# Up projection of a decoder block on one core: where the second 1/rms lives, and the order of some products and evictions

## The chip, the cores and the metric

One core of a Trainium2 chip runs the whole kernel in one launch. The metric is the device time of that launch in microseconds; where several runs are shown, their median counts. A profile is one execution of its own, with its own time, and its trace begins at the first instruction. TensorE (PE) multiplies, VectorE (DVE), ScalarE (ACT) and GpSimd (POOL) do the element-wise work, and SyncE (SP) issues most of the transfers. All matrix data are 32-bit floats, held for the products as a rounded high part and a low part.

## The reference, cut to what matters

```
x  = x + g1 * mix                                  # (1024 tokens, 1024 features)
h2 = rmsnorm(x, norm2_g) * (1 + sc2) + sh2         # 1/rms over the features of each token
u  = h2 @ w_up                                     # 1024 -> 2 * 2816
u  = causal_dwconv(u, conv_ffn_w)                  # 3 taps along the tokens
ff = silu(gate) * val                              # u split in two halves of 2816
x  = x + g2 * (ff @ w_down)
```

Everything ahead of the first line (a short convolution and an attention, merged by gates, and the product `mix` itself) has been done by other stages; the change lies between the end of `mix` and the first blocks of `u`.

## The kernel before

Activations are kept transposed: features on the 128 partitions (8 feature tiles, ND = 8, in two groups of NK = 4), tokens along the row, in two halves of 512 (`lo` and `hi`). A product of two 32-bit operands is three products of their parts: high by high, high by low, low by high. So one output block of 128 by 512 over 4 feature tiles is 12 products of TensorE.

**The output projection.** `mix_mm(e, w, halves)` (L1400) sums the product of feature tile e in an accumulator, and `mix_end(m)` (L1406) evicts it: one DVE instruction adds it, times the gate, to `x1[e]`, ACT squares the result, POOL adds the square to a running sum `sqs` (for the last feature tile, e = 7, the square stays in a tile of its own, `sq7`), and SP stores `x1[e]` to DRAM. For e = 4 to 7 the first token half is done first and the second half after it, so that the norm of the first half runs beside the products of the second.

**The norm of one half.** `norm2_sum` (L1422) sums the squares over the features: 8 products with one column of ones (16 entries on TensorE), then four small DVE and ACT instructions for 1/rms, and four that write diagonal matrices `diag`. `norm2_spread` (L1434) multiplies ones by them (4 products, 8 entries), which leaves 1/rms of each token on all partitions in a PSUM bank `pb`. `norm(e, g, pb)` (L1439) scales `x1[e]` in place by it, and `split_h` on ACT (L1444) and `split_l` on DVE (L1450) make the high and low part of the operand. The operands of the first half are B11 and B21, of the second B12 (its tile is named T4, since T4 takes its place later) and B22. `h2_chain` (L1494) does norm and split of the first half step by step, between the evictions of `mix`.

**The up projection.** Output tiles of 128 features come in pairs, a gate and a value block per `Up` object: `u.g` and `u.v`, each an accumulator of two PSUM banks (1024 columns). The first three, u0, u1 and u2, use plain products: `u.plain(n, half)` (L1577) is one block of 12 products; bit 0 of n says gate or value, bit 1 which group of feature tiles. From the fourth on a scheme with seven products in place of eight is used; its operands T1 to T3 are made by `t_sums` and `t_op` (L1716, L1726) on DVE and ACT while TensorE works on the plain products, and T4 (in the place of B12) when u2 has read B12. Weight tiles are fetched by `up_fetch` and split in high and low by `plain_split` (L1516): ACT writes `wh`, DVE `wl`. Splits 0 and 1 (`wsp[0:2]`) are u0's gate and value, 2 and 3 u1's, 4 and 5 u2's.

**What sets the order.** For PE, DVE, ACT and POOL the order of the instructions is that of the program text (a `manual_schedule` block); each engine takes its own in that order. SP's transfers are ordered by the scheduler. PSUM is eight banks, all of them held by `acc4` (L1291): four buffers of two banks, taken in rotation, and a new tile in a buffer waits until the last user of the old one is done. The 1/rms of the second half has no buffer of its own: before the change it lies in the `hi` half of u1.v,

```
    pst = pb = u1.v[:, hi]
```

and u1's products for the first token half, which write `u1.v[:, lo]`, come in the program ahead of the loop that reads `pb`.

Of the kernel before, what the change touches and what calls it, by code (L numbers as in the profile page):

```python
# [33 lines left out]
def tile_hybrid_block(  # L34
# [51 lines left out]
    def wsplit(fetched, eng=vector, pool=None):  # L86

        ws, n, m = fetched
        if pool:
            wh, wl = (pool.tile([P, 1040], F32R, tag=nm, name=nm, bufs=2) for nm in ("wh", "wl"))  # L90
        else:
            wh, wl = wtile("wh"), wtile("wl")
        scalar.activation(wh[:, : n * m], ws[:, : n * m], AF.Copy)  # L93
        eng.tensor_tensor(out=wl[:, : n * m], in0=ws[:, : n * m], in1=f32(wh[:, : n * m]), op=ALU.subtract)  # L94
        return tuple(t[:, : n * m].rearrange("p (n m) -> p n m", n=n) for t in (wh, wl))
# [5 lines left out]
    def mac(acc, wh, wl, xh, xl, halves, start, stop):  # L101

        n = 512
        terms = ((wh, xh), (wh, xl), (wl, xh))
        for t, (w, xx) in enumerate(terms):
            for hf in halves:
                sl = slice(hf * n, hf * n + n)
                mm(acc[:, sl], w, xx[:, sl], start=start and t == 0, stop=stop and t == 2)
# [36 lines left out]
    NK = ND // 2  # L145
    lo, hi = slice(0, 512), slice(512, 1024)
# [15 lines left out]
    def newton_rsqrt(pool, v, n, nm, root_of=None):  # L162


        s = pool.tile([P, n], F32, tag="nr_s", name=nm + "s", bufs=2)
        y = pool.tile([P, n], F32, tag="nr_y", name=nm + "y", bufs=2)
        t = pool.tile([P, n], F32, tag="nr_t", name=nm + "t", bufs=2)
        r = pool.tile([P, n], F32, tag="nr_r", name=nm + "r", bufs=2)
        if root_of:
            scalar.activation(s, root_of[0], AF.Sqrt, scale=root_of[1], bias=epst)  # L170
        else:
            scalar.activation(s, v, AF.Sqrt)
        vector.reciprocal(y, s)
        vector.scalar_tensor_tensor(out=t, in0=v, scalar=-0.5, in1=y, op0=ALU.mult, op1=ALU.mult)
        vector.tensor_tensor(out=t, in0=t, in1=y, op=ALU.mult)
        vector.scalar_tensor_tensor(out=r, in0=t, scalar=1.5, in1=y, op0=ALU.add, op1=ALU.mult)
        return r
# [406 lines left out]
    def small(nm):  # L584
        return bp.tile([P, NT * NH], F32, name=nm)

    z = zf.rearrange("p a b -> p (a b)")
    nz, u, w, lw, m, num, den, lf = (small(n) for n in "nz u w lw m num den lf".split())
# [702 lines left out]
    def acc4(nm):  # L1291
        return psD.tile([P, S], F32, tag="acc", name=nm, bufs=4)
# [50 lines left out]
    wmix = {}  # L1343
# [56 lines left out]
    def mix_mm(e, w, halves, ks=range(ND), acc=None):  # L1400
        acc = acc or acc4("mix")
        for k in ks:
            mac(acc, w[0][:, k, :], w[1][:, k, :], mH[:, k, :], mL[:, k, :], halves, k == 0, k == ND - 1)
        return e, acc, halves

    def mix_end(m):  # L1406

        e, acc, halves = m
        sl = slice(512 * halves[0], 512 * halves[-1] + 512)
        vector.scalar_tensor_tensor(out=x1[e][:, sl], in0=acc[:, sl], scalar=g1[:, e : e + 1], in1=x1[e][:, sl],  # L1410
                                    op0=ALU.mult, op1=ALU.add)
        for g in halves:
            src = x1[e][:, hsl[g]]
            if e in (0, ND - 1):
                scalar.activation(sq7 if e else sqs[g], src, AF.Square)
            else:
                sq = ep.tile([P, 512], F32, tag="sq", name="sq", bufs=2)
                scalar.activation(sq, src, AF.Square)
                gpsimd.tensor_tensor(out=sqs[g], in0=sqs[g], in1=sq, op=ALU.add)
        sync.dma_start(x1_d[e, :, sl], x1[e][:, sl])  # L1420

    def norm2_sum(g, pst):  # L1422

        for i in range(4):
            for t, sq in enumerate((sqs[g], sq7)):
                mm(pst[:, i : i + 1], sq[:, i * P : (i + 1) * P], ones[:, 0:1], start=t == 0, stop=t == 1)
        v = up.tile([P, 4], F32, tag="v2", name="v2", bufs=2)
        vector.tensor_scalar(out=v, in0=pst[:, 0:4], scalar1=1.0 / D, scalar2=EPS, op0=ALU.mult, op1=ALU.add)
        r = newton_rsqrt(up, v, 4, "r2")
        for i in range(4):  # L1430
            vector.tensor_scalar(out=diag[:, i * P : (i + 1) * P], in0=ident, scalar1=r[:, i : i + 1], scalar2=None,
                                 op0=ALU.mult)

    def norm2_spread(pb):  # L1434

        for i in range(4):
            mm(pb[:, i * P : (i + 1) * P], ones, diag[:, i * P : (i + 1) * P], start=True, stop=True)
# [12 lines left out]
    def split_l(dst, kk, src, bias=None, eng=vector):  # L1450
        if bias is None:
            eng.tensor_tensor(out=dst[1][:, kk], in0=src, in1=f32(dst[0][:, kk]), op=ALU.subtract)
        else:
            vector.scalar_tensor_tensor(out=dst[1][:, kk], in0=src, scalar=bias, in1=f32(dst[0][:, kk]), op0=ALU.add,
                                        op1=ALU.subtract)
# [11 lines left out]
    for e in range(4):  # L1467
        if e < 2:
            m = mix_mm(e, wmix[e], (0, 1), (ND - 2, ND - 1), ms[e][1])
        else:  # L1470
            m = mix_mm(e, wmix[e], (0, 1))
# [7 lines left out]
    def up_fetch():  # L1479

        n = len(raw)
        raw.append(wfetch(kview(w_up[0], (n // 2 + n % 2 * NF) * P, P), 8, P))

    for e in range(4, ND):
        m = mix_mm(e, wmix[e], (0,))
# [8 lines left out]
    def h2_chain():  # L1494

        for e in range(ND + 2):
            if e < ND:
                norm(e, 0, pb)
            if 1 <= e <= ND:
                d = e - 1  # L1500
                t, bias = x1[d][:, lo], b2[:, d : d + 1]
                if d < NK:
                    split_h(B11, d, t, bias)
                else:
                    scalar.activation(t, t, AF.Identity, bias=bias)
                    split_h(B21, d - NK, t)
            if e >= 2:
                d = e - 2
                t, bias = x1[d][:, lo], b2[:, d : d + 1]
                if d < NK:  # L1510
                    split_l(B11, d, t, bias)
                else:
                    split_l(B21, d - NK, t)
            yield

    def plain_split():  # L1516

        wsp.append(wsplit(raw[len(wsp)]))
        if len(raw) < 2 * N0:
            up_fetch()  # L1520

    wsp = []
    m = mix_mm(4, wmix[4], (1,), range(4))
    norm2_sum(0, acc4("st"))
    m = mix_mm(4, wmix[4], (1,), range(4, ND), m[1])
    pb = acc4("pb")[:, lo]
    norm2_spread(pb)
    mix_end(m)
    chain = h2_chain()
    m = mix_mm(5, wmix[5], (1,))  # L1530
# [4 lines left out]
        next(chain)  # L1535
    mix_end(m)
    m = mix_mm(6, wmix[6], (1,))
    for _ in chain:
        pass
    plain_split()  # L1540
    mix_end(m)
    m = mix_mm(7, wmix[7], (1,))
    plain_split()
    mix_end(m)
    eS.close()
    xbS.close()
    mS.close()
# [184 lines left out]
    def norm_low(e):  # L1732
        split_l((B12, B22)[e // NK], e % NK, x1[e][:, hi], b2[:, e : e + 1])

    u0, u1, u2 = U[:N0]
    for u in (u0, u1):
        u.v, u.g = (acc4(nm) for nm in ("upv", "upg"))
    u0.xs = wsp[0:2]
    pst = pb = u1.v[:, hi]
    u0.plain(0, 0)  # L1740
    plain_split()
    u1.xs = wsp[2:4]
    norm2_sum(1, pst)
    u0.plain(1, 0)
    u0.plain(2, 0)
    norm2_spread(pb)
    u0.plain(3, 0)
    for n in range(4):
        u1.plain(n, 0)
    for e in range(ND):  # L1750
        norm(e, 1, pb)
        split_h((B12, B22)[e // NK], e % NK, x1[e][:, hi], b2[:, e : e + 1])
        if e:
            norm_low(e - 1)
    norm_low(ND - 1)
    for n in (0, 2, 1, 3):
        u0.plain(n, 1)
    for n in (0, 1, 2, 3):
        u1.plain(n, 1)
    for kk in range(NK):  # L1760
# [20 lines left out]
            u0.ff_out()  # L1781
            U[3].fetch(up)
    u2.xs = wsp[4:6]
    u2.v, u2.g = (acc4(nm) for nm in ("upv", "upg"))
    for n in (0, 2, 1, 3):
        for half in range(2):
            u2.plain(n, half)
# [16 lines left out]
    for f in range(N0, NF):  # L1804
        u, bf = U[f], U[f - 1]
# [69 lines left out]
    class Step:  # L1875
# [40 lines left out]
        def mm(self, banks, es=range(4)):  # L1916
            for e in es:
                es_ = slice(e * P, (e + 1) * P)
                for t, (i, j) in enumerate(((0, 0), (0, 1), (1, 0))):
                    mm(banks[e], self.A[i][:, es_], self.B[j], start=self.p in FIRST and self.c == 0 and t == 0,  # L1920
                       stop=self.c == NC - 1 and t == 2, skip_group_check=True)
# [55 lines left out]
    u = U[NF - 1]  # L1977
# [8 lines left out]
    for t, st in enumerate(steps[: len(steps) - NE + 1]):  # L1986
        n = t // NC
# [81 lines left out]
```

## Time and profile before

| | us |
|---|---|
| median of 3 runs (1484.1, 1484.42, 1488.18) | 1484.42 |
| the profiled execution, whole | 1484.04 |
| its span, from the first to the last instruction | 1482.3 |
| TensorE busy | 1405.8 (95%) |
| VectorE busy | 1101.4 (74%) |
| ScalarE busy | 652.7 (44%) |
| GpSimd busy | 503.9 (34%) |

The mean granted TensorE clock is 0.989 of full speed. The stretch that the change touches runs from about 770 us (the last evictions of `mix`) to about 860 us (the first products of u2). A row of a timeline gives the start, the duration, the engine, the line, the operation, the tiles, and in brackets the idle time of the engine before it with the instruction that released it. Matmuls overlap: the pace is the distance of their starts, not their duration.

### The profile page before, as it was taken

The numbers are of one execution on the slowest core, as the hardware profiler recorded it, in microseconds if no ns is written. First come the engines' busy times: TensorE is split into PE (matmuls) and PEld (weight loads), VectorE is DVE, ScalarE is ACT, GpSimd is POOL, SyncE is SP. The second block draws the span as 40 slices with busy tenths as digits, with TensorE's granted clock in tenths as the row PEclk, the third lists the DMA queues.
The fourth block names the chain that finished last, engine by engine and source line by source line (L and its number), as shares of the span: only waits on it lengthen the run. The fifth ranks groups of instructions, "written<-read, shape, count | busy, mean of one in ns | idle before, by whom it ended". The sixth has DMA issues, their size and how long they took to land. (4 is left out here: it accounts for less than half of the span.)

```text
span 1482.3 us, 19374 instructions
## 1 busy us (share of the span) xinstructions
PE 1405.8 (95%) x6668; PEld 1155.2 (78%) x6668; DVE 1101.4 (74%) x1828; ACT 652.7 (44%) x1104; POOL 503.9 (34%) x532
## 2 busy tenths in 40 slices
PE   5889789999999999899999899999999999999997
PEld 4679668887888888678787677888888888888875
DVE  7965798987777776457745678778777786898764
ACT  6454453434555454555323343333333333444443
POOL 3646566655555553313121013333333331000000
PEclk9999999999999999999999999999999999999999
DMA  9539654537655557675952032222222213983622
GB/s 285 158 113 329 194 148 128 151 94 205 162 159 126 147 133 250 193 272 205 240 138 86 0 100 86 85 86 86 85 85 72 70 44 109 390 317 106 214 79 72
DMA packets 260760, 222.45 MB, mean 150 GB/s; under 512 B 43117, under 2 KB 213445, under 8 KB 260661
## 3 DMA queue, kind: packets, MB, share of 16 engines
q1 hardware_dynamic: 259389, 218.61, 49.2%
q0 software_dynamic: 1136, 2.56, 0.6%
q8 instruction: 53, 0.87, 0.3%
q14 instruction: 46, 0.38, 0.1%
q10 hardware_dynamic: 136, 0.04, 0.0%
HBM read 169.76 MB, written 51.41 MB: 149 GB/s over the span
## 5 line engine op out<-in xcount | busy, mean ns | idle before, releaser
L1920 PE MATMUL dn<-bL,aH 128*128 128x512 f32 x308 | 120.3, 391 | 0.6 <-DVE bL L1914 0.6
L1920 PE MATMUL dn<-bH,aH 128*128 128x512 f32 x308 | 120.9, 392 | 0.0
L1920 PE MATMUL dn<-bH,aL 128*128 128x512 f32 x308 | 120.0, 390 | 0.0
L1557 ACT ACTIVATE wh<-ws 128x512 fp32r<-128x512 f32 x95 | 55.5, 627 | 133.7 <-POOL ws L1591 130.9
L730 DVE TENSOR_TENSOR ol<-ws,oh 128x512 fp32r<-128x512 f32 x98 | 94.8, 976 | 14.6 <-ACT oh L729 11.3
L94 DVE TENSOR_TENSOR wl<-ws,wh 128x1024 fp32r<-128x1024 f32 (+1 forms) x51 | 69.5, 1363 | 41.3 <-ACT wh L93 41.3
L729 ACT ACTIVATE oh<-ws 128x512 fp32r<-128x512 f32 x98 | 61.3, 626 | 71.6 <-PE pacc L775 38.4
L1591 POOL TENSOR_TENSOR ws<-ws 128x512 f32<-128x512 f32 x19 | 24.6, 1293 | 195.0 <-DVE wl L94 195.0
L1162 ACT ACTIVATE L<-L,mn 128x256 f32<-128x256 f32 (+6 forms) x56 | 46.5, 830 | 60.4 <-DVE mn L1160 58.5
L1165 POOL TENSOR_SCALAR L<-L,rs 128x384 f32<-128x384 f32 (+7 forms) x62 | 48.7, 786 | 70.2 <-DVE rs L1164 68.5
L1920 PEld LDWEIGHTS dn<-bL,aH 128*128 128x128 f32 x308 | 57.8, 188 | 13.8 <-DVE bL L1914 2.0
L1185 ACT ACTIVATE th<-pt 128x512 fp32r<-128x512 f32 (+1 forms) x80 | 43.8, 551 | 56.2 <-PE pt L1179 54.5
L559 POOL TENSOR_TENSOR ws<-ws 128x512 f32<-128x512 f32 x42 | 55.1, 1311 | 36.4 <-DVE ol L730 16.9
L1920 PEld LDWEIGHTS dn<-bH,aH 128*128 128x128 f32 x308 | 57.8, 188 | 12.3 <-ACT bH L1913 0.4
L1920 PEld LDWEIGHTS dn<-bH,aL 128*128 128x128 f32 x308 | 57.8, 188 | 11.9
L93 ACT ACTIVATE wh<-ws 128x1024 fp32r<-128x1024 f32 (+1 forms) x58 | 60.8, 1051 | 13.3 <-DMA ws<-in_w_branch_a_dram 5.1
L1558 DVE TENSOR_TENSOR wl<-ws,wh 128x512 fp32r<-128x512 f32 x76 | 64.2, 863 | 2.3 <-ACT wh L1557 2.3
L1913 ACT ACTIVATE aH<-dws 128x512 fp32r<-128x512 f32 x52 | 32.8, 631 | 74.6 <-issue 41.0
L1186 DVE TENSOR_TENSOR tl<-pt,th 128x512 fp32r<-128x512 f32 (+1 forms) x80 | 50.5, 634 | 18.8 <-ACT th L1185 17.4
L1678 DVE SCALAR_TENSOR_TENSOR u<-upv,cwT,u 128x1023 f32<-128x1023 f32 (+1 forms) x44 | 56.4, 1281 | 10.7 <-ACT u L1674 10.0
L439 POOL TENSOR_TENSOR wacc<-wacc,wa 128x256 f32<-128x256 f32 x48 | 43.3, 903 | 56.0 <-ACT wa L438 53.0
L1914 DVE TENSOR_TENSOR aL<-dws,aH 128x512 fp32r<-128x512 f32 x52 | 35.8, 689 | 34.3 <-ACT aH L1913 34.3
(564 smaller groups left out, 4506.9 us busy)
## 6 DMA issues: line engine op xcount, KB each, us to landing
wa<-in_w_ada_dram SPq DMA_DIRECT2D x48, 512.0 KB
dws<-in_w_down_dram SPq DMA_DIRECT2D x96, 256.0 KB
ws<-in_w_up_dram SPq DMA_DIRECT2D x44, 512.0 KB
ws<-in_w_in_dram SPq DMA_DIRECT2D x36, 512.0 KB
ff<-ff_d SPq DMA_DIRECT2D x44, 256.0 KB
ff_d<-u SPq DMA_DIRECT2D x21, 512.0 KB
xt<-in_x_dram SPq DMA_DIRECT2D x8, 512.0 KB
v_d<-vt SPq DMA_DIRECT2D x8, 512.0 KB
```

Of the source, the lines that this page charges most:

```text
L93: scalar.activation(wh[:, : n * m], ws[:, : n * m], AF.Copy)
L94: eng.tensor_tensor(out=wl[:, : n * m], in0=ws[:, : n * m], in1=f32(wh[:, : n * m]), op=ALU.subtract)
L559: gpsimd.tensor_tensor(out=o, in0=a, in1=b, op=ALU.subtract)
L729: scalar.activation(h, src, AF.Copy)
L730: eng.tensor_tensor(out=l, in0=src, in1=f32(h), op=ALU.subtract)
L1162: scalar.activation(L[:, :n], L[:, :n], AF.Exp, scale=-1.0, bias=mn, accum_out=sm)
L1165: eng.tensor_scalar(out=L[:, :n], in0=L[:, :n], scalar1=rs, scalar2=0.0, op0=ALU.mult, op1=ALU.add)
L1186: vector.tensor_tensor(out=flat[2][:, c0:], in0=flat[0][:, c0:], in1=f32(flat[1][:, c0:]), op=ALU.subtract)
L1557: scalar.activation(ops[0][:, sl], src, AF.Copy)
L1558: eng.tensor_tensor(out=ops[1][:, sl], in0=src, in1=f32(ops[0][:, sl]), op=ALU.subtract)
L1678: vector.scalar_tensor_tensor(out=u[:, s:], in0=acc[:, : S - s], scalar=cwT[:, 2 - s, n : n + 1], in1=u[:, s:], op0=ALU.mult, op1=ALU.add)
L1920: mm(banks[e], self.A[i][:, es_], self.B[j], start=self.p in FIRST and self.c == 0 and t == 0, stop=self.c == NC - 1 and t == 2, skip_grou ...
```

## The change

The second half's 1/rms gets an accumulator of its own, `norm_ps`: the sum goes to its first bank, the spread to its second. It takes the next buffer of the rotation, so u1.v becomes the fifth tile and shares the buffer of `norm_ps`. The loop that normalises the second half stands directly behind the spread, with the fourth weight split inside it (after its sixth feature tile). u0's blocks for the second half come ahead of the two blocks that write u1.v's first half, and in the order 0, 1, 2, 3. Gate and value tiles are created in the other order. At the end of `mix`, the eviction of feature tile 6 comes after three steps of the chain and not at its end, and the eviction of tile 7 ahead of the third weight split.

```diff
     m = mix_mm(6, wmix[6], (1,))
+    for _ in range(3):
+        next(chain)
+    mix_end(m)
     for _ in chain:
         pass
     plain_split()
+    m = mix_mm(7, wmix[7], (1,))
     mix_end(m)
-    m = mix_mm(7, wmix[7], (1,))
     plain_split()
-    mix_end(m)
...
     u0, u1, u2 = U[:N0]
-    for u in (u0, u1):
-        u.v, u.g = (acc4(nm) for nm in ("upv", "upg"))
-    u0.xs = wsp[0:2]
-    pst = pb = u1.v[:, hi]
+    norm_ps = acc4("pb")
+    u0.g, u0.v, u1.g, u1.v = (acc4(nm) for nm in ("upg", "upv", "upg", "upv"))
+    u0.xs, u1.xs = wsp[0:2], wsp[2:3]
     u0.plain(0, 0)
-    plain_split()
-    u1.xs = wsp[2:4]
-    norm2_sum(1, pst)
+    norm2_sum(1, norm_ps[:, lo])
     u0.plain(1, 0)
-    u0.plain(2, 0)
+    pb = norm_ps[:, hi]
     norm2_spread(pb)
-    u0.plain(3, 0)
-    for n in range(4):
-        u1.plain(n, 0)
     for e in range(ND):
         norm(e, 1, pb)
         split_h((B12, B22)[e // NK], e % NK, x1[e][:, hi], b2[:, e : e + 1])
         if e:
             norm_low(e - 1)
+        if e == NK + 1:
+            plain_split()
+            u1.xs = wsp[2:4]
     norm_low(ND - 1)
-    for n in (0, 2, 1, 3):
+    u0.plain(2, 0)
+    u0.plain(3, 0)
+    u1.plain(0, 0)
+    u1.plain(2, 0)
+    for n in (0, 1, 2, 3):
         u0.plain(n, 1)
+    u1.plain(1, 0)
+    u1.plain(3, 0)
     for n in (0, 1, 2, 3):
         u1.plain(n, 1)
...
-    u2.v, u2.g = (acc4(nm) for nm in ("upv", "upg"))
+    u2.g, u2.v = (acc4(nm) for nm in ("upg", "upv"))
```

## Rows read from the trace of the kernel before

**Rows 1.** The page, busy time of TensorE: us, share of the span, instructions.

```profile
PE   1405.8 (95%) x6668; PEld 1155.2 (78%) x6668; DVE 1101.4 (74%) x1828; ACT 652.7 (44%) x1104; POOL 503.9 (34%) x532
```

**Rows 2.** Windows: length, busy us of each engine, granted clock, DMA share, GB/s.

```profile
776.50:778.30 1.80, 1.80 (x18) 1.75 (x17) 0.00 (x0) 0.19 (x1) 0.00 (x0) 1.00 0.00 0
...
801.40:804.90 3.50, 1.89 (x17) 1.80 (x16) 1.86 (x3) 1.57 (x2) 0.00 (x0) 0.99 0.66 196
804.90:808.10 3.20, 3.20 (x10) 2.52 (x10) 2.15 (x10) 0.21 (x1) 0.00 (x0) 0.50 0.84 262
812.00:827.00 15.00, 15.00 (x70) 12.05 (x68) 0.00 (x0) 0.00 (x0) 0.00 (x0) 1.00 0.00 1
827.00:838.80 11.80, 7.78 (x26) 4.10 (x26) 11.45 (x18) 5.73 (x9) 0.00 (x0) 1.00 0.00 0
```

**Rows 3.** Waits of TensorE, 798 to 860 us: us, times, longest.

```profile
PE upv L1426 <- ACT U L1415: 1.6, 1, 1.6
PE upg L1567 <- ACT T4H L1448: 1.6, 1, 1.6
...
PE upg L1567 <- DVE wl L94: 0.3, 1, 0.3
```

**Rows 4.** Timeline of TensorE, both norm sums and the plain products.

```profile
776.57 0.28 PE L1426 MATMUL st<-ones,sqs 128*128 128x1 f32 x2
...
778.28 0.48 PE L108 MATMUL mix<-mH,wh 128*128 128x512 f32 x1
...
781.16 1.05 PE L1437 MATMUL pb<-U,ones 128*128 128x128 f32 x8
781.96 0.48 PE L108 MATMUL mix<-mH,wh 128*128 128x512 f32 x1
...
798.61 0.39 PE L1567 MATMUL upg<-B11H,wh 128*128 128x512 f32 x1
...
801.40 0.28 PE L1426 MATMUL upv<-ones,U 128*128 128x1 f32 x2
...
804.92 0.77 PE L1567 MATMUL upv<-B11H,wh 128*128 128x512 f32 x1
...
809.31 0.39 PE L1567 MATMUL upg<-B21H,wh 128*128 128x512 f32 x1
...
826.62 0.40 PE L1567 MATMUL upv<-B21H,wl 128*128 128x512 f32 x1
...
838.77 0.40 PE L1567 MATMUL upv<-T4H,wh 128*128 128x512 f32 x1
...
855.37 0.39 PE L1567 MATMUL upg<-B11H,wh 128*128 128x512 f32 x1
...
858.71 0.39 PE L1567 MATMUL upg<-T4H,wh 128*128 128x512 f32 x1
```

**Rows 5.** Timeline of VectorE: a weight split, two evictions, the second norm.

```profile
785.39 1.22 DVE L94 TENSOR_TENSOR wl<-ws,wh 128x1024 fp32r<-128x1024 f32 x1 [0.42 <-ACT wh L93]
...
797.92 0.75 DVE L1410 SCALAR_TENSOR_TENSOR x<-mix,mod,x 128x512 f32<-128x512 f32 x1
...
801.84 0.74 DVE L1410 SCALAR_TENSOR_TENSOR x<-mix,mod,x 128x512 f32<-128x512 f32 x1
...
806.59 0.87 DVE L1431 TENSOR_SCALAR U<-ident,r2r 128x128 f32<-128x128 f32 x4
827.05 1.41 DVE L1442 SCALAR_TENSOR_TENSOR x<-x,a,upv 128x512 f32<-128x512 f32 x2 [19.59 <-PE upv L1567]
...
836.52 1.63 DVE L1454 SCALAR_TENSOR_TENSOR B22L<-x,mod,B22H 128x512 fp32r<-128x512 f32 x2
```

**Rows 6.** Timeline of ScalarE: a weight split, and the start of T4.

```profile
784.32 1.04 ACT L93 ACTIVATE wh<-ws 128x1024 fp32r<-128x1024 f32 x1
...
870.74 2.69 ACT L1446 ACTIVATE T4H<-x 128x512 fp32r<-128x512 f32 x4 [11.52 <-PE upv L1567]
```

**Rows 7.** Timeline of SP's queue: the store of x1[7], second half.

```profile
802.61 0.35 SPq L1420 DMA_DIRECT2D x_d<-x  x1
```

## The prediction, made before the changed kernel was run

> **What bounds the kernel now.** I read the page first: TensorE is busy 95% of the span [rows 1], so only what lets TensorE stand or run slowly can be won. Then its waits in the stretch of the change, then its timeline there, and last the timelines of the engines that release it. Between 798 and 860 us it waits for the last square, for the first T4 part, for the parts after it, and for a weight split [rows 3]. The pace of its undisturbed products comes from one row pair: from 838.77 to 855.37 there are six blocks of 12, 72 products, in 16.60 us, 0.2306 us each, so 2.77 us a block [rows 4].
>
> Three places of this stretch are slower than that.
>
> First, the second sum of squares. Its products begin at 801.40 and stand until the square of feature tile 7 is there [rows 3]; u0's next block begins at 804.92, 3.52 us later [rows 4]. The first half's sum is the same work with nothing to wait for: 776.57 to 778.28, 1.71 us [rows 4]. The square is late because its eviction is: DVE evicts tile 6 at 797.92 and tile 7 at 801.84 [rows 5], although TensorE had ended tile 7 when u0 began at 798.61 [rows 4]. In the program's order a weight split stands ahead of each.
>
> Second, the clock: right after that stretch it is granted at 0.50, the 1.2 GHz level, from 804.9 to 808.1 [rows 2], and the block from 804.92 to 809.31 takes 4.39 us [rows 4].
>
> Third, the second norm. The diagonals are ready at 806.59 + 0.87 = 807.46, but DVE stands 19.59 us until 827.05, released by a product into upv [rows 5]. The last product into u1.v's `lo` half starts at 826.62 and takes 0.40 [rows 4]: 827.02. So the read of `pb`, which was complete long before, waits for products into the other bank of the same tile. When it goes, the products of the second half follow DVE one feature tile at a time: two blocks, 24 products, hold TensorE from 826.62 + 0.23 = 826.85 to 838.77 [rows 4], with 7.78 us busy of 11.80 [rows 2].
>
> **The change part by part.** No product, split or transfer is added or removed; everything is order and place. The sum is made in the profiled execution (span 1482.3, whole time 1484.04, 0.38 under the median of the runs, 1484.42).
>
> *The evictions of mix.* Tile 6's eviction now comes after three chain steps, tile 7's ahead of the third split. Tile 6 moves ahead of the chain's last low part and the second split (ACT 1.04, DVE 1.22 [rows 5, 6]); that split moves behind tile 6's square, about 0.8 us later, and is first needed by u0's second block at 803. Tile 7 can be evicted when its products end, about 798.8; with the eviction (0.74) and the square (before, the eviction ended at 802.58 and the sum's 1.71 us, counted back from 804.92, began at 803.21: 0.63) it is there by 800.2, and the sum starts at 801.40: a margin of 1.2 us. The wait goes: 3.52 − 1.71 = **−1.81 us**. If tile 7 came as late as before, this term would be 0, and nothing makes it worse than before. Split 3 now follows the square and is ready about 802.7; u1's first block needs it at 812.
>
> *The clock.* Without the stand, sum, one block and spread are what the first half had: 1.71 us, 12 products in 2.88 (778.28 to 781.16), spread 0.80 (to 781.96) [rows 4], and the clock was 1.00 over that sum [rows 2]. I take the first half's block: 4.39 − 2.88 = **−1.51 us**. The other end is 0 (the clock falls again).
>
> *The spread with one block ahead of it and not two.* The chain from sum to diagonals took 807.46 − 804.92 = 2.54 us [rows 4, 5], the block takes 2.88: the cover is 0.34 us thinner than I would like, but it holds. The fourth split, which stood ahead of this chain on ACT and DVE, is no longer there. Without that cover the price is the missing part, between 0 and 2.54; the first half, with exactly this order, has no gap. I take 0.
>
> *The norm loop.* It now stands behind the spread alone. TensorE's new times: sum 801.40 to 803.11, block to 805.99, spread to 806.79, four more blocks for the first half (one starts 0.08 late after the spread, as 2.88 against 2.77 shows) to 817.95; then u0's second half: its T4 blocks from 817.95, its first B22 block from 823.49, its end at 829.03; u1's six remaining blocks to 845.65. DVE starts the loop at 805.99 + 1.05 = 807.04. Before, the loop ran from 827.05 to 836.52 + 1.63 = 838.15, 11.10 us or 1.39 a feature tile [rows 5]. The four T4 pairs are thus ready about 807.1 + 5 × 1.39 = 814, four us before use. The fourth split inside the loop, with ACT idle and then DVE, costs at most 1.04 + 1.22 = 2.26 [rows 5, 6], so the loop ends by 820.4, three us before the first B22 block. If those covers were gone, TensorE would pay the missing part us by us. u1.v must wait for the loop (same buffer): 820.4 against its first block at 829.03. So the paced stretch becomes two plain blocks: 838.77 − 826.85 = 11.92 against 24 × 0.2306 = 5.53, **−6.39 us**.
>
> *Behind it.* The T1 to T3 work on DVE and ACT begins 838.15 − 820.4 = 17.7 us earlier, while u2's first block begins 9.7 earlier. That block took 858.71 − 855.37 = 3.34 us, since it met a split not yet ready [rows 3, 4]; with eight us more lead that goes: 3.34 − 2.77 = **−0.57 us**. The next thing on ACT, T4, waits for TensorE's reading of B12 (11.52 us idle before 870.74 [rows 6]), so from there all engines move with TensorE, and the small waits after it stay as they are. U[3]'s fetch waits for the buffer of the fourth split, which comes free some 12 us later than before (about 817 against 805), and its first readers come after T4, which is to start near 860: a cover of over 40 us. Gate and value tiles in the other order only exchange which buffer is free first.
>
> Sum: −1.81 − 1.51 − 6.39 − 0.57 = **−10.28 us**: 1473.8 for the profiled execution, **1474.1** as a median.
>
> **Rivals.**
>
> *The clock still falls at the second sum.* For it: it fell here once [rows 2], and 1.7 us of one-column products remain. Against: the same sum in the first half left it at 1.00 [rows 2]. Price 1.51: 1475.7. The Trainium skill ("TensorE: Matmul & The Clock Gate", Part 1, "What's actually happening") says that "the default state is throttled, and activity releases the throttle"; by that a dull stretch is enough, even without a stand, and the time would be this rival's; the trace shows one case either way.
>
> *The loop still waits for products, by whatever rule the wait was made.* If norm were released only after the fourth block behind the spread, at 818.4 and not 807.1, it would end at 818.4 + 11.10 + 2.26 = 831.8, u0's first B22 block about 0.7 later, at 832.5 and not 826.26. That loses 6.2 of the 10.28: 1480.3. For it: the 19.59 us. Against: in the new program no product stands between spread and loop.
>
> *Slower: the store of x1[7].* The loop overwrites x1[7] in place, so it must wait until the store of its second half has read it. Before, the store was issued at 802.61 [rows 7] and the overwrite came about 836; now 799.6 and about 818.3. A store landing at X puts the B22 block's end at about X + 2.8; from X = 823.5 it costs time, from X = 833.7 (34 us after its issue) it eats the whole gain, and at 40 us the time would be 1490. For it: SP's order is the scheduler's and may put weight loads ahead. Against: DMA share is 0.00 from 812 to 827 [rows 2], so all had landed within 9.4 us.
>
> *The wait only changes its place,* because the DVE and ACT work behind the loop, not the loop, ends last: then u2 begins where it did, 1484.4. Against: DVE is idle those 19.59 us, and the change gives them to exactly this work.
>
> **How the numbers follow.** Forecast 0.82 (1474.1), clock 0.10 (1475.7), late loop 0.04 (1480.3), wait moved 0.01 (1484.4), store 0.03 (1490). A measurement tells about 0.3%, 4.45 us, from no change: faster means under 1479.97. The first two are faster, 0.92; the next two within, 0.05; the last slower, 0.03. The range: at the low end the forecast less 1.8 us, for runs that differ and for small waits behind 860 that I left as they are; at the high end the clock rival and as much again: 1472.3 to 1477.5.
>
> **What would show it.** Right: no wait of TensorE at the second sum; granted clock 1.00 throughout from 798 to 860; DVE's first norm of the second half right behind the spread, near 807; no wait for T4 or B22 parts; u2's first product near 845.6; and everything behind it moved by one amount, about 10.3. Wrong: a new wait of TensorE in front of the spread, in front of u1.v's first block or for the third or fourth split, or 0.50 after the sum. The forecast fails if the DVE loop starts after 811 (its margin of four us gone), or if the time won by 846 is lost again behind 860.

## The result, and the profile after

The changed kernel takes 1473.59 us (median of 4 runs, 1471.79 to 1476.64) against 1484.26 of the kernel before in the same rounds (median of 4). The ratio is 0.9925, with a 95% interval of 0.9908 to 0.9942: between 8.6 and 13.7 us less. The forecast was 1474.1 in a range of 1472.3 to 1477.5.

| profiled execution | before | after |
|---|---|---|
| whole | 1484.04 | 1473.5 |
| span | 1482.3 | 1471.5 |
| TensorE busy | 1405.8 | 1403.4 |

The busy time of TensorE hardly changed (2.4 us): most of what went is time in which it stood. Up to the change the two executions agree by luck: the second sum of squares begins at 801.40 before and at 801.38 after, so the two timelines can be laid on each other by their times. Here is TensorE's timeline of the changed kernel, from that sum to u2's second block; it answers to the second half of [rows 4]. The row of the kernel before in which the sum stood is given ahead of it.

```profile
803.29 1.77 PE L1426 MATMUL upv<-ones,U 128*128 128x1 f32 x14 [1.61 <-ACT U L1415]
```

```profile
801.38 1.84 PE L1426 MATMUL pb<-ones,U 128*128 128x1 f32 x16
803.09 0.48 PE L1569 MATMUL upv<-B11H,wh 128*128 128x512 f32 x1
...
805.94 1.05 PE L1437 MATMUL pb<-U,ones 128*128 128x128 f32 x8
806.75 0.48 PE L1569 MATMUL upg<-B21H,wh 128*128 128x512 f32 x1
...
817.90 0.40 PE L1569 MATMUL upg<-T4H,wh 128*128 128x512 f32 x1
...
829.05 0.39 PE L1569 MATMUL upv<-B11H,wh 128*128 128x512 f32 x1
...
845.74 0.39 PE L1569 MATMUL upg<-B11H,wh 128*128 128x512 f32 x1
...
848.54 0.39 PE L1569 MATMUL upg<-T4H,wh 128*128 128x512 f32 x1
```

All 16 entries of the sum now stand in one row without a gap (before there were 2, a stand, and 14). The block behind it takes 805.94 − 803.09 = 2.85 us and not 4.39. u0's second half begins at 817.90 and u2 at 845.74 (855.37 before). The windows of the same stretch, with columns as in [rows 2]:

```profile
801.40:803.20 1.80, 1.80 (x18) 1.80 (x17) 1.23 (x1) 0.02 (x1) 0.00 (x0) 1.00 0.99 314
803.20:806.00 2.80, 2.80 (x14) 2.29 (x14) 1.71 (x9) 0.20 (x1) 0.00 (x0) 1.00 0.69 210
806.00:818.00 12.00, 12.00 (x58) 9.96 (x57) 9.75 (x14) 5.63 (x8) 0.00 (x0) 1.00 0.01 2
818.00:829.00 11.00, 11.00 (x49) 8.90 (x48) 10.63 (x17) 4.57 (x7) 0.00 (x0) 1.00 0.17 48
```

The first two numbers of each row are equal: TensorE is busy all the time. The granted clock (third number from the right) is 1.00 throughout. VectorE's timeline shows why; it answers to [rows 5]: the two evictions, the diagonals, the loop's first norm and its last low parts.

```profile
795.15 0.74 DVE L1410 SCALAR_TENSOR_TENSOR x<-mix,mod,x 128x512 f32<-128x512 f32 x1
...
799.07 0.74 DVE L1410 SCALAR_TENSOR_TENSOR x<-mix,mod,x 128x512 f32<-128x512 f32 x1
...
804.50 0.88 DVE L1431 TENSOR_SCALAR U<-ident,r2r 128x128 f32<-128x128 f32 x4
807.03 1.41 DVE L1442 SCALAR_TENSOR_TENSOR x<-x,a,pb 128x512 f32<-128x512 f32 x2 [1.65 <-PE pb L1437]
...
818.81 1.62 DVE L1454 SCALAR_TENSOR_TENSOR B22L<-x,mod,B22H 128x512 fp32r<-128x512 f32 x2
```

The loop is released by the spread (line 1437 into pb) after 1.65 us of idle time, in place of 19.59 and a product into upv. Both evictions come 2.8 us earlier. From 740 to 1300 us, into the down projection, these waits of TensorE are left (total, times, longest), besides one of 0.3 us in the down projection:

```profile
PE upv L1569 <- ACT s L1633: 1.3, 1, 1.3
PE upv L1569 <- ACT wh L93: 0.9, 1, 0.9
PE upg L1569 <- DVE U L1625: 0.6, 1, 0.6
PE upv L1569 <- DVE wl L1560: 0.6, 1, 0.6
PE upv L1569 <- DVE wl L94: 0.5, 1, 0.5
```

They are those that the kernel before had behind T4; all waits of [rows 3] are gone.

### The profile page after: what moved, and what is told of

Same layout as the page of the kernel before. It is cut to its first block, busy times and chain, and to the rows that moved or that the text cites. A ratio compares the mean times of both kernels' runs of the same rounds, so it can differ in the third digit from the quotient of the medians.

```text
span 1471.5 us, 19375 instructions
## 1 busy us (share of the span) xinstructions
PE 1403.4 (95%) x6668; PEld 1155.1 (78%) x6668; DVE 1099.4 (75%) x1828; ACT 651.8 (44%) x1104; POOL 504.1 (34%) x532
## 5 line engine op out<-in xcount | busy, mean ns | idle before, releaser
L1680 DVE SCALAR_TENSOR_TENSOR u<-upv,cwT,u 128x1023 f32<-128x1023 f32 (+1 forms) x44 | 56.4, 1282 | 10.7 <-ACT u L1676 9.9
```

What stands on the lines that cost most here:

```text
L1680: vector.scalar_tensor_tensor(out=u[:, s:], in0=acc[:, : S - s], scalar=cwT[:, 2 - s, n : n + 1], in1=u[:, s:], op0=ALU.mult, op1=ALU.add)
```

## The experiments

The time of one execution differs by some us from the next, and most of it ahead of the change: in the ten profiles of the table below the second sum begins between 797.98 and 803.73 us. So beside the ratio of whole times I give the length of the affected stretch in each profile: from the first product of the second sum to the first product with bL in the down projection. For before and after it is read from the sum's row (801.40 in [rows 4], 801.38 above) and the first time in these two rows, of before and of after (durations shortest, median and longest in ns, then first and last start):

```profile
L1920 PE MATMUL dn<-bL,aH x308: 387/389/504, 1252.0 to 1474.6; 128*128 128x512 f32 x154
```

```profile
L1925 PE MATMUL dn<-bL,aH x308: 387/389/504, 1242.0 to 1464.9; 128*128 128x512 f32 x154
```

| kernel | median us | ratio to before (95%) | stretch us | against before |
|---|---|---|---|---|
| before | 1484.4 and 1483.9 | 1 | 450.6 | |
| after | 1473.59 | 0.9925 (0.9908 to 0.9942) | 440.6 | −10.0 |
| after, again | 1474.30 | 0.9928 (0.9913 to 0.9944) | 440.6 | −10.0 |
| 1: evictions only | 1481.39 | 0.9979 (0.9966 to 0.9991) | 447.3 | −3.3 |
| 2: norm only | 1477.64 | 0.9953 (0.9935 to 0.9970) | 444.0 | −6.6 |
| 3: shared tile | 1474.73 | 0.9934 (0.9915 to 0.9953) | 440.6 | −10.0 |
| 4: loop two blocks earlier | 1477.20 | 0.9954 (0.9940 to 0.9968) | 445.6 | −5.0 |
| 5: no block under the root | 1477.15 | 0.9950 (0.9935 to 0.9964) | 443.9 | −6.7 |
| 6: work ahead of T4 | 1467.25 | 0.9881 (0.9861 to 0.9900) | 434.9 | −15.7 |
| 7: split 4 ahead | 1473.39 | 0.9924 (0.9902 to 0.9946) | 440.6 | −10.0 |

Each ratio is taken to the kernel before in the same rounds: 1484.26 for the first row of the changed kernel, 1484.4 for experiments 1 to 4, 1483.9 for 5 to 7 and the changed kernel again.

My theory was that three causes add up: the late square, the low clock that the stand in front of it brings, and the loop's wait for products that have nothing to do with it.

**The changed kernel again**, as the measure of the others.

> The changed kernel once more, on the chip and in the rounds of the other three, as their measure: 10 to 10.7 us less than before, and in its profile 440.6 us from the first product of the second sum to the first product of the down projection.

The stretch is 440.6 again (799.78 to 1240.4); the whole time is 9.6 us under before in those rounds, a little less than the 10 to 10.7 expected, which lie within its interval (8.3 to 12.9). The stretch repeats to a tenth of a us where the whole time does not; that is why the experiments are read by it.

**1: the evictions alone.** The kernel before, with

```diff
     m = mix_mm(6, wmix[6], (1,))
+    for _ in range(3):
+        next(chain)
+    mix_end(m)
     for _ in chain:
         pass
     plain_split()
+    m = mix_mm(7, wmix[7], (1,))
     mix_end(m)
-    m = mix_mm(7, wmix[7], (1,))
     plain_split()
-    mix_end(m)
```

> The kernel before with the new order of the last mix evictions alone; the second 1/rms still lies in u1.v. Theory (three separate causes that add up): the square of tile 7 comes before the sum, so the stand of 1.6 us goes, and with it the stretch at clock 0.50, since it was the stand that let the clock fall: 1.81 + 1.51 = 3.3 us less than before. DVE still waits some 19.6 us for the loop, and the paced stretch of 11.92 us stays. Rival (the one-column products alone let the clock fall): 0.50 stays after the sum, 1.8 us less. Rival (the stretch is bound by the loop's wait, so that what is won ahead of it is lost in it): no change.

The stretch is 3.3 us shorter, as the theory had it. In TensorE's timeline the sum is one row, and VectorE still waits in front of the loop, 17.83 us and not the 19.6 expected, since the products that hold it now end earlier behind the sum:

```profile
803.73 1.84 PE L1426 MATMUL upv<-ones,U 128*128 128x1 f32 x16
```

```profile
826.03 1.40 DVE L1442 SCALAR_TENSOR_TENSOR x<-x,a,upv 128x512 f32<-128x512 f32 x2 [17.83 <-PE upv L1569]
```

The clock behind the sum, as a window:

```profile
805.40:808.60 3.20, 3.20 (x16) 2.64 (x16) 2.40 (x10) 0.21 (x1) 0.00 (x0) 1.00 0.79 234
```

It is 1.00, where the kernel before had 0.50 for the same products. So the first rival, that the one-column products alone let the clock fall, is out, and with it the prediction's reading that a dull stretch is enough even without a stand; and what was won ahead of the loop's wait was not lost in it.

**2: the norm alone.** The changed kernel with the old order of the evictions (the diff of experiment 1 taken back).

> The changed kernel with the old order of the last mix evictions. Theory: the stand in front of the second sum (1.6 us) and the clock of 0.50 behind it are back, so block u0(1,0) takes about 4.4 us again; the loop still starts right behind the spread, and the paced stretch is gone. Against before 10.1 - 3.3 = 6.8 us less. Rival (the evictions are needed for the loop to be in time): TensorE waits for T4 or B22 parts and less than 5 us is won.

6.6 us, against 6.8 expected; with the 3.3 of experiment 1 that makes 9.9 of the 10.0. The stand is back, and the clock with it:

```profile
802.74 1.72 PE L1426 MATMUL pb<-ones,U 128*128 128x1 f32 x14 [1.64 <-ACT U L1415]
```

```profile
804.40:807.50 3.10, 3.10 (x9) 2.44 (x9) 1.70 (x9) 0.21 (x1) 0.00 (x0) 0.52 0.36 127
```

TensorE waits for no T4 or B22 part: the loop is in time without the evictions. The two hunks are independent.

**3: the tile of its own taken away.** The changed kernel with

```diff
-    norm_ps = acc4("pb")
     u0.g, u0.v, u1.g, u1.v = (acc4(nm) for nm in ("upg", "upv", "upg", "upv"))
+    norm_ps = u1.v
```

> The changed kernel with the 1/rms of the second half in u1.v as before (sum in its first bank, spread in its second), all orders as in the change: no tile of its own. Theory (what holds the loop is the products into the same tile that stand ahead of it in the program; behind the loop they do no harm): same as the changed kernel, 10 us less than before, the loop starts near 807 us. Rival (the tile of its own is what frees the loop): DVE waits again for products into upv, about 820 or later, TensorE waits for T4 and B22 parts, and at most 4 us less than before is left.

The stretch is that of the changed kernel to a tenth, and the loop starts right behind the spread, though it reads from upv:

```profile
803.63 1.41 DVE L1442 SCALAR_TENSOR_TENSOR x<-x,a,upv 128x512 f32<-128x512 f32 x2 [1.65 <-PE upv L1437]
```

The rival falls: with the new order, the tile of its own gives no time. What frees the loop is that it stands ahead of the blocks that write u1.v. The other way round, a tile of its own with the loop left in its old place, was not run.

**4: the loop only two blocks earlier.** The kernel before, 1/rms in u1.v, with

```diff
-    for n in range(4):
+    for n in (0, 2):
         u1.plain(n, 0)
     for e in range(ND):
         norm(e, 1, pb)
...
     norm_low(ND - 1)
+    for n in (1, 3):
+        u1.plain(n, 0)
     for n in (0, 2, 1, 3):
         u0.plain(n, 1)
```

> The kernel before, 1/rms still in u1.v, with one move: the loop stands ahead of the two blocks that write u1.v, but still behind three blocks into other tiles (u0(3,0), u1(0,0), u1(2,0)). It tells by which rule the loop waited. Theory (by tile): the loop starts right behind the spread, near 813.2, runs beside those three blocks, and the first block into u1.v waits until the loop's last read, near 822.8, 1.5 us after TensorE could have begun it; u2 begins near 850.5 and 5.4 us less than before are measured. Rival (by place in the program: whatever product stands ahead holds it): the loop starts near 821.3, TensorE stands for the whole loop (some 9.8 us), and the kernel is about 3 us slower than before.

The loop is released by the spread although three blocks into other tiles stand between the two in the program, and the first block into u1.v waits for the loop's last read, by the 1.5 us expected:

```profile
811.57 1.41 DVE L1442 SCALAR_TENSOR_TENSOR x<-x,a,upv 128x512 f32<-128x512 f32 x2 [5.73 <-PE upv L1437]
```

```profile
819.37 0.39 PE L1567 MATMUL upg<-B21H,wl 128*128 128x512 f32 x1
821.28 0.47 PE L1567 MATMUL upv<-B11H,wh 128*128 128x512 f32 x1 [1.52 <-DVE x L1442]
821.58 0.39 PE L1567 MATMUL upv<-B11L,wh 128*128 128x512 f32 x1
```

5.0 us are won, 5.4 were expected. The starts around this wait lie 1.91 apart and the next two 0.30, where undisturbed products are 0.23 apart: the wait cost 1.91 − 0.23 + 0.07 = 1.75 and not 1.5, which is 0.2 of the missing 0.4; the rest was not followed. So the waits of this program go by the tile, in both directions: in the kernel before the read waited 19.59 us for products that stand ahead of it into the other bank of its PSUM tile, and here a product waited 1.52 us for reads of the other bank. Place in the program alone does not hold the loop, and the kernel did not become slower.

**5: nothing beside the chain to the diagonals.** The changed kernel with

```diff
     norm2_sum(1, norm_ps[:, lo])
-    u0.plain(1, 0)
     pb = norm_ps[:, hi]
     norm2_spread(pb)
+    u0.plain(1, 0)
```

> The changed kernel with the spread directly behind the sum of squares: block u0(1,0), which lay beside the chain from the sum to the diagonals, comes after the spread. Theory (the block covers the chain; a stand among such small products lets the clock fall): TensorE stands some 1.7 us in front of the spread, the clock is granted at 0.50 for some 3 us after it, and the kernel takes 3.2 us more than the changed one. Rival (the clock fell in the kernel before for another reason): it stays at 1.00, and 1.7 us more are measured.

The stretch is 3.3 us longer than the changed kernel's, 3.2 were expected. TensorE stands 1.62 us in front of the spread, and the next block runs at half the clock:

```profile
806.89 1.59 PE L1437 MATMUL pb<-U,ones 128*128 128x128 f32 x8 [1.62 <-DVE U L1431]
```

```profile
808.10:810.80 2.70, 2.70 (x8) 2.16 (x8) 2.15 (x4) 1.38 (x2) 0.00 (x0) 0.50 0.00 0
```

**7: the fourth split back ahead of the sum.** The changed kernel with

```diff
     u0.plain(0, 0)
+    plain_split()
+    u1.xs = wsp[2:4]
     norm2_sum(1, norm_ps[:, lo])
...
-        if e == NK + 1:
-            plain_split()
-            u1.xs = wsp[2:4]
```

> The changed kernel with the fourth weight split back ahead of the second sum instead of inside the loop. Theory (both places are covered): the chain from the sum to the diagonals becomes some 0.5 us longer and ends just within the block beside it, the loop ends 2.2 us earlier with nobody waiting for it: same time as the changed kernel within 0.2 us. Rival (the split in the chain's way is why it was moved): TensorE waits in front of the spread, 0.5 us or more, and the clock may fall, up to 2 us more.

Same stretch, 440.6. The diagonals end at 804.90 + 0.88 = 805.78, the spread starts at 805.88 with nothing to wait for:

```profile
804.90 0.88 DVE L1431 TENSOR_SCALAR U<-ident,r2r 128x128 f32<-128x128 f32 x4
```

```profile
805.88 1.05 PE L1437 MATMUL pb<-U,ones 128*128 128x128 f32 x8
```

So the split's new place buys nothing but margin: 0.1 us here, 0.56 in the changed kernel (805.94 − 805.38).

**6: work moved ahead of T4.** In the changed kernel ACT stands 19.14 us in front of T4, which waits for TensorE's last reading of B12, with u1's end and the fourth block's first split queued behind it:

```profile
860.64 2.73 ACT L1446 ACTIVATE T4H<-x 128x512 fp32r<-128x512 f32 x4 [19.14 <-PE upv L1569]
```

The five waits listed above all come within 30 us of that row. The changed kernel with

```diff
+    u1.scale_g()
+    U[3].x_split()
+    u1.taps_g()
+    u1.silu()
+    U[3].sums13()
+    U[3].split3()
+    U[3].sum2()
     for kk in range(NK):
         t_op(kk, 3, False)
         t_op(kk, 3, True)
-    u1.scale_g()
     u1.scale_v()
-    u1.taps_g()
-    u1.silu()
-    U[3].x_split()
     u1.taps_v()
     u1.ff()
     u1.ff_out()
     U[4].fetch(up)
-    U[3].sums13()
-    U[3].split3()
-    U[3].sum2()
     u2.scale_g()
```

> The changed kernel with one more move: u1's gate scale, taps and silu and the fourth block's first weight split, sums and split of the difference (ACT, DVE and GpSimd work) stand ahead of T4, whose wait for TensorE leaves ACT idle for 19.1 us and DVE for 11.4. Theory (the five waits of TensorE behind T4, 0.9 + 0.5 + 1.3 + 0.6 + 0.6 = 3.9 us, come from work queued behind T4): all five go, 3.3 to 3.9 us less than the changed kernel, 13.5 to 14 us less than before. Rival (the value block's taps, which must stay behind T4, are what is late): only the first two go, 1.5 us less.

All five waits are gone: TensorE has one wait between 740 and 1300 us, 0.3 us in the down projection. But the stretch is 5.7 us shorter than the changed kernel's, more than either theory allowed. The size of the waits was misread. In the changed kernel:

```profile
869.16 0.50 PE L1569 MATMUL upv<-B11H,wh 128*128 128x512 f32 x1 [0.87 <-ACT wh L93]
869.50 0.40 PE L1569 MATMUL upv<-B11L,wh 128*128 128x512 f32 x1
870.42 0.50 PE L1569 MATMUL upv<-B11H,wl 128*128 128x512 f32 x1 [0.53 <-DVE wl L94]
870.76 0.40 PE L1569 MATMUL upv<-B11H,wh 128*128 128x512 f32 x1
```

The second wait is listed with 0.53, yet the starts around it lie 0.92 apart, and the next product again 0.34 and not 0.23: it cost 0.92 − 0.23 + 0.11 = 0.80. The product ahead is drawn with 0.40 us, to 869.90, and only what comes after that is listed as idle; and the first product after the wait takes 0.11 more than the pace. The same sum of starts over that stretch, with two short gaps that no wait is listed for, gives 5.6 us, and in experiment 6's own rows of that stretch no such gap is left. At 1467.25 us and a ratio of 0.9881 this version beats both kernels.

Two parts of the change were not run alone: the order 0, 1, 2, 3 of u0's second half, and the exchange of the gate and value tiles.

## Why the prediction was right, step by step

*The late square.* Forecast −1.81; measured 803.09 − 801.38 = 1.71 for the sum, so −1.81. The reading that the weight splits ahead of the evictions made it late is shown by experiments 1 and 2.

*The clock.* Forecast −1.51; the block took 2.85, so −1.54. The rival (it falls again) had 0.10; it did not, and experiment 5 shows what brings it back.

*The spread with one block ahead.* Forecast 0 with 0.34 us of margin, by the slow chain of before; the measured margin was 0.56, since the chain ran at 804.50 + 0.88 − 803.09 = 2.29.

*The norm loop.* Forecast: start 807.04, end 820.4, u0's second half at 817.95, u2 at 845.65. Measured: 807.03, 818.81 + 1.62 = 820.43, 817.90 and 845.74. The fourth split's price inside the loop was 2.30 us (the loop took 13.40 against 11.10; 2.26 had been taken as the most), and nobody waited for it. At u2 the changed kernel is 53.97 − 44.36 = 9.61 us ahead, counted from the start of the sum (855.37 − 801.40 and 845.74 − 801.38); less 1.81 and 1.54 for the sum and its block that leaves 6.26 for this term, against 6.39. The rivals of a late loop and of a wait that only changes its place are out by these times. The mechanism was half a step off in its words: I named the place of `pb` in u1.v's tile and the place of the loop together. Experiments 3 and 4 separate them: the tile is the rule by which the wait is made, the order is enough to remove it.

*u2's first block.* Forecast −0.57; it took 848.54 − 845.74 = 2.80 against 3.34, so −0.54.

*Behind it.* T4 begins 10.10 us earlier (860.64 against 870.74 in [rows 6]), the down projection 10.0. The last eviction of all came 9.67 us earlier, read in these two rows of before and after:

```profile
1476.67 0.38 ACT L1962 ACTIVATE ot<-dn 128x256 f32<-128x256 f32 x1 [0.37 <-PE dn L1956]
```

```profile
1467.00 0.38 ACT L1967 ACTIVATE ot<-dn 128x256 f32<-128x256 f32 x1 [0.37 <-PE dn L1961]
```

So of the forecast 10.28 some 10.1 were there at T4 and 9.7 at the end; the 0.4 between lie in stretches that the change does not touch and I did not follow them. That the span shrank by 10.8 is due to its tail: from that eviction to the end there were 5.6 us before and 4.5 after. This part of the agreement is luck of one execution, not the forecast's.

*The slower rival.* The store of x1[7] was issued at 799.84 (forecast 799.6):

```profile
799.84 0.35 SPq L1420 DMA_DIRECT2D x_d<-x  x1
```

The DMA share from 806 to 818 is 0.01 in the window above, so it had landed before the loop's last norm, and the loop shows no wait there.

## What to carry to other kernels

A read whose data are complete can still be held by work on another part of its tile: look up which product the idle time names, and whether it stands ahead of the reader in the program. Moving the reader ahead of it was enough here (experiments 3 and 4); whether a buffer of its own would do it without the move, no run shows. Read what a wait of TensorE costs as the distance of the starts around it less one pace, restart included, and not as the idle time in brackets.

## What the runs showed of the hardware that was not expected

The 1.7 us of one-column products did not lower the granted clock by themselves. In four profiles TensorE stood about 1.6 us in or behind the 1.7 us of one-column products (before, experiments 2, 4 and 5), and in all four the clock was at the 1.2 GHz level (0.50 to 0.52) for the next three us. In the six without the stand (after, after again, 1, 3, 6 and 7) it was 1.00 in the same place. So a stand of 1.6 us cost 3.3 us there. A stand of the same length did not lower it elsewhere: in the kernel before TensorE stood 1.59 us between 512-column products,

```profile
828.61 0.50 PE L1567 MATMUL upg<-T4H,wh 128*128 128x512 f32 x1 [1.59 <-ACT T4H L1448]
```

and the clock was 1.00 from 827 to 838.8 [rows 2]. The stand and the one-column products beside it came together in all four profiles with the low clock; neither alone had it between 798 and 900 us.

The first product after a wait also took longer than the pace: 0.34 us to the second one in the rows of experiment 6, 0.30 in those of experiment 4, against 0.23.
